# Which engine makes the low parts of the streamed weights in a four-layer decoder trunk

## Chip, core and metric

The kernel runs on one core of one Trainium2 chip. The metric is the device time of one execution in microseconds (us); lower is better.

## What is computed

Four layers act on one sequence of 256 tokens with 1024 features in float32. Each layer normalises its input, runs a token mixer of its own kind (sparse attention in three branches, differential, dilated and stick-breaking attention), gates the result with a SiLU path, projects it back, normalises it again and adds it to the running state.

```python
def reference(x, norm_pre, norm_post, a_w_in, a_w_out, ...):
    h = x
    for i in range(DEPTH):                       # DEPTH = 4
        m, j = i % N_MIXERS, i // N_MIXERS
        u = rms_norm(h, norm_pre[i])
        if m == 0:
            y = nsa_mixer(u, a_w_in[j], a_w_out[j], ...)
        elif m == 1:
            y = diff_mixer(u, b_w_in[j], b_w_out[j], ...)
        elif m == 2:
            y = dilated_mixer(u, c_w_in[j], c_w_out[j])
        else:
            y = stick_mixer(u, d_w_in[j], d_w_out[j])
        h = h + rms_norm(y, norm_post[i])
    return h
```

Every mixer ends in `(o * silu(z)) @ w_out`, and q, k, v and z come from `u @ w_in`. These projections are most of the matrix work.

## The kernel before

**Weights as a stream.** All projection weights come from HBM in 164 pieces of at most 128 x 1024 float32, in the order of their use (the list `seq`). Layer 0 has its v pieces, its other input pieces, eight pieces of a small network that are not split, and its output pieces; layers 1 to 3 follow with eight v pieces (`b_v`, `c_v`, `d_v`), 20 or 24 further input pieces (`b_t`, ...) and eight output pieces (`b_o`, ...).

**The split.** A float32 product is made of three products of a shorter format (fp32r): an operand is written as a high part plus a low part, and the product low times low is left out. `advance` (L70 to L115) starts the DMA of a piece into one of five `raw` buffers, has ScalarE copy it into the high part `whi` (L106), and then subtracts, `wlo = raw - whi` (L108). The high and low parts lie in eleven buffers each. Which engine makes the subtraction is the choice `on_pool` (L107): VectorE (`DVE`), or GpSimd (`POOL`) for piece 6, for the pieces of the table `POOL2`, and for the fifth and eighth v piece of layers 1 to 3 (`POOLV`). In `POOL2` are six pieces near the end of layer 0 (29, 33, 37, 41, 45 and 49, the last of which is the second v piece of layer 1) and three at the end of layer 3 (152, 156 and 160). Without piece 6 that makes 15 pieces. TensorE multiplies the activations with the parts in `mm3` (L202 to L204) and `nat` (L262 to L264).

**Order of the work.** TensorE's order is written out by hand. On the other engines a scheduler sorts by priority; the splits from piece 12 on have a low one (`LATE`), so that the order of an engine is fixed when the program is built, and depends on which instructions the engine has. An engine works through its list strictly in order.

**From one layer to the next** (three times; "boundary" in what follows). The output projection (`out_proj`) does token block 0, then token block 1. While TensorE works on block 1, block 0 is normalised and transposed. When block 1's projection is done, a chain of small steps follows: squares on ScalarE (L417), mean (L421) and product (L423) on VectorE, a power on GpSimd (L157), the addition to `h` (L435, two halves), again squares (L173 on ScalarE, L174 on VectorE), L176, again a power on GpSimd (L157), scaling (L183, two halves), and then the transposes on TensorE (L190), after which ScalarE and VectorE write `uth` and `utl` (L193, L194). Meanwhile TensorE does the v projection of block 0 for the next layer (16 steps of three matmuls, L262 to L264), and the transposes of block 1 are placed before its fourteenth and before its last step (`with_trans`). The eight v pieces are split in this same stretch.

**Layer 3.** A unit handles two heads: scores on TensorE, L1031 on VectorE, three ScalarE passes (L1032, L998), L1035, two scans (L1038) and L1040 on VectorE, an exponential on ScalarE, transposes on TensorE (L303), copies to SBUF on ScalarE (L148), and the product with v on TensorE (L319, L322). VectorE does the two heads one after the other, with splits in between.

Of the kernel before, what the change touches and what calls it, by code (L numbers as in the profile page):

```python
# [17 lines left out]
PSUM = bass.MemoryType.PSUM  # L18
# [8 lines left out]
KO = (0, 4, 1, 5, 2, 6, 3, 7)  # L27
X1AT, SUMAT, UAT, T1AT, WARM = 4, 1, 3, 4, 12
POOLED = (6,)
POOL2 = (*range(29, 50, 4), *range(152, 164, 4))  # L30
POOLV = (("_v", 4), ("_v", 7))
CHAIN, T0, T1, V0, V1 = 400, 6, 4, 3, 1


# [5 lines left out]
def trunk(ctx, tc, I, out):  # L40
# [7 lines left out]
    ps = ctx.enter_context(tc.tile_pool(name="ps", bufs=1, space=PSUM))  # L48
    ctx.enter_context(tc.manual_schedule(engines={mybir.EngineType.PE}))

# [1 line left out]
    seq = []  # L52

    def add(name, *idx, split=True):
# [14 lines left out]
    raw, parts = {}, {}  # L69

    def advance(most=len(seq)):
        while True:
            while st["load"] < min(len(seq), st["split"] + NS - st["held"] + max(0, min(3, 8 - st["split"]))):
                i = st["load"]
                if i == X1AT:
                    nc.sync.dma_start(h[:, 1, :], I["x"][1])
                _, k, c = seq[i][0].shape
                if 5 <= i < 8:
                    if i == 5:
                        st["extra"] = big.tile([128, 3, 560], F32, name="oT")  # L80
                    t = st["extra"][:, i - 5, :]
                else:
                    t = wts.tile([128, 1024], F32, name="raw", bufs=NS)[:, :k * c]
                t = t.rearrange("p (k c) -> p k c", k=k)
                dma = nc.sync.dma_start(t, seq[i][0])
                if i == 7:
                    st["dma"] = dma.ins
                raw[i] = t
                st["load"] += 1
            i = st["split"]  # L90
            if i >= st["load"] or st["parts"] >= NH or i >= min(most, st["most"]):
                return
            t = raw.pop(i)
            st["split"] += 1
            if not seq[i][1]:
                parts[i] = t
                st["held"] += 1
                continue
            _, k, c = seq[i][0].shape
            hi, lo = [wts.tile([128, 1024], F32R, name=n, bufs=NH)[:, :k * c].rearrange("p (k c) -> p k c", k=k)  # L100
                      for n in ("whi", "wlo")]
            with ExitStack() as after:
                after.enter_context(tc.high_priority(offset=LATE if i >= 12 else 0))
                for ins in st["after"]:
                    after.enter_context(tc.issue_after(ins))
                ACT.activation(hi, t, AF.Copy)  # L106
                on_pool = i in POOLED or i in POOL2 or (i > 8 and seq[i][2] in POOLV)  # L107
                lo_of = (POOL if on_pool else DVE).tensor_tensor(lo, t, hi.bitcast(F32), op=OP.subtract)  # L108
                if i == max(POOLED):
                    st["pool"] = lo_of.ins  # L110
                elif not on_pool:
                    st["lo"] = lo_of.ins
            parts[i] = (hi, lo)
            st["parts"] += 1
# [7 lines left out]
            parts.pop(i)  # L122
            st["parts" if seq[i][1] else "held"] -= 1

# [1 line left out]
    def bcast_load(dst, name, l):  # L126
        src = I[name]
        nc.scalar.dma_start(dst, bass.AP(tensor=src.tensor, offset=src.offset + l * D, ap=[[0, 128], [1, D]]))
# [5 lines left out]
    nc.scalar.dma_start(gcol, I["gain0"])  # L134
    ident = const.tile([128, 128], F32, name="ident")

# [1 line left out]
    cnt = {"ev": 0}  # L138

    def evac(dst, src, eng=None):  # L140
# [67 lines left out]
    ready = {}  # L208

    def fill():  # L210
        """Work of the queue between two attention steps, spread evenly over the steps that are left."""
        n = -(-(len(fq) - plan["keep"]) // max(1, plan["slots"]))
        plan["slots"] -= 1
        for _ in range(max(0, n)):
            pop()
# [7 lines left out]
            pop()  # L223

    def need(i):
        """Projection i and a little more, so that its result has left PSUM."""
        while fq and (i not in ready or plan["count"] < ready[i] + 6):
            pop()

    def push_proj(use, q=fq, idx=None):  # L230
        """Two streamed pieces -> [128 cols, 2, 256 tokens] in PSUM, given to use()."""
        t = {}
        idx = idx or take(2)

        def step(c, k):
            if c == 0 and k == 0:
                t["o"] = ps.tile([128, 2, 256], F32, name="mm", bufs=NMM)
            wh, wl = parts[idx[c]]
            mm3(t["o"][:, c, :], wh[:, k, :], wl[:, k, :], uT[0][:, k, :], uT[1][:, k, :], k == 0, k == 7)
            if k == 7:  # L240
                free(idx[c])
                if c == 1:
                    use(t["o"])
                advance()

        for c in range(2):
            for k in range(8):
                q.append(lambda c=c, k=k: step(c, k))

    def nat(stat, b, idx, c0, c1, use, last, ko=range(8)):  # L250
        """Natural orientation: token block b, columns c0:c1 of 8 kt in the pieces idx; a list of steps."""
        t = {}

        def step(k):
            if k == 0:
                t["o"] = ps.tile([128, 512], F32, name="mm", bufs=NMM)
            o = t["o"][:, 0:c1 - c0]
            i, j = divmod(k, 8 // len(idx))
            wh, wl = parts[idx[i]]
            bs = slice(b * 128, (b + 1) * 128)  # L260
            sh, sl = stat[0][:, ko[k], bs], stat[1][:, ko[k], bs]
            PE.matmul(o, sh, wh[:, j, c0:c1], start=k == 0, stop=False)  # L262
            PE.matmul(o, sl, wh[:, j, c0:c1], start=False, stop=False)  # L263
            PE.matmul(o, sh, wl[:, j, c0:c1], start=False, stop=k == 7)  # L264
            if k == 7:
                use(o)
                if last:
                    free(*idx)
                    advance()

        return [lambda k=k: step(k) for k in range(8)]

    def with_trans(steps, trans, t0, t1):
        """The transposes of the other token block go in near the end of the steps."""
        n = len(steps)
        if trans:
            steps[n - t0:n - t0] = trans[0:1]
            steps[n + 1 - t1:n + 1 - t1] = trans[1:2]
        for f in steps:
            f()  # L280

    def v_proj(trans):
        """Token block 0 first; trans: the transposes that bring in token block 1."""
        v = big.tile([128, 2, D], F32, name="v")
        idx = take(8)
        for b in range(2):
# [19 lines left out]
        return t  # L306

    def scores(S, kT, qT, kc, qc, halves):
        """S[j] [128, 384] = q block 0 x keys 0..127 | q block 1 x keys 0..255, heads on partition halves."""
        for b in range(2):  # L310
            for j in halves:
                r = slice(64 * j, 64 * j + 64)
                PE.matmul(S[j][:, 128 * b:128 * b + 128 * (b + 1)], qT[r, qc, b * 128:(b + 1) * 128],  # L313
                          kT[r, kc, 0:128 * (b + 1)], start=True, stop=True)

    def pv_pair(o, PT, v, cols, first, last):
        """o [128 = 2 heads x 64, 256 tokens] += V^T P^T; PT[j], cols[j] for the two heads."""
        for j in range(2):
            PE.matmul(o[64 * j:64 * j + 64, :], v[:, 0, cols[j]:cols[j] + 64], PT[j][:, 0:256],  # L319
                      start=first, stop=False)  # L320
# [2 lines left out]
                      start=False, stop=last)  # L323

    class Gate:
        """g = o * silu(z) in two fp32r parts; column tiles 2i, 2i+1 once o and z are both there."""

        def __init__(self, scale, silu):
            self.scale, self.silu, self.w, self.o, self.gh = scale, silu, {}, set(), None
# [32 lines left out]
                DVE.tensor_tensor(lo, g, hi.bitcast(F32), op=OP.subtract)  # L362

        def open(self):
            """The scores are done: the query and key tiles take the two parts of g."""
            self.gh = [big.tile([128, 8, 256], F32R, name=n) for n in ("qT", "kT")]
            for i in range(self.ready):
                self.split(i)

    def pipeline(units, ga, pattern, keep=8, tail=3):  # L370
        """units: (fronts, backs) of closures; the fronts of unit n + 1 go with the backs of unit n."""
        n = len(units)
        order = []
        for i in range(n + 1):
# [100 lines left out]
        return [a.ins, v.ins]  # L475

    def start(steps):
        """Layer 0's first projection as x and the weights come in; steps[k]: both column chunks of k, block 0."""
        make_identity(nc, ident)
        uT[0] = big.tile([128, 8, 256], F32R, name="uth")  # L480
        uT[1] = big.tile([128, 8, 256], F32R, name="utl")
# [68 lines left out]
    nc.sync.dma_start(cq, I["qscale"])  # L550
    causal = mask_tile("causal")

    # =================== layer 0: native sparse attention ===================
    SLA = slopes_of(16)
    pos = const.tile([128, 2, 16], F32, name="pos")
    nc.sync.dma_start(pos, I["pos"])
# [153 lines left out]
    CS, PTC = {}, {}  # L710

    def cmp_front(g):
        """Compressed branch, the 4 heads of a group at once."""
        need(g)
        sc = ps.tile([128, 512], F32, name="S", bufs=NSB)
        for b in range(2):
# [91 lines left out]

    trans = out_proj(pipeline([nsa_unit(p) for p in range(8)], ga, "FFBFBBB"), 0)

    # =================== layer 1: differential attention ===================
    SLB = slopes_of(8)
    LI = 0.8 - 0.6 * math.exp(-0.3)
    lamt = work.tile([128, 384], F32, name="P", bufs=8)[:, 0:256].rearrange("p (a b) -> p a b", a=4)
# [101 lines left out]

    trans = out_proj(pipeline([diff_unit(hd) for hd in range(8)], ga, "FBFBFBB"), 1)

    # =================== layer 2: dilated attention ===================
    SLC = slopes_of(12)  # L920
    with tc.issue_after(st["pool"]):
        masks = [mask_tile("near"), mask_tile("by4"), mask_tile("by16")]
# [62 lines left out]

    trans = out_proj(pipeline([dilated_unit(hg) for hg in range(4)], ga, "FFBFBB"), 2)

    # =================== layer 3: stick-breaking attention ===================
    with tc.issue_after(st["pool"]):
        mstrict = mask_tile("strict")  # L990
        zero = const.tile([128, 256], F32, name="zero")
# [64 lines left out]

# [1 line left out]
def _nat(w, nk=(2, 2, 2, 2), nc_=512):  # L1058
    """[1024, C] -> pieces [128, kt, nc_] for each column chunk, split over kt."""
    import numpy as np  # L1060
    w = w.reshape(8, 128, w.shape[1])
    res = []
# [6 lines left out]


def _tr(w):
    """[1024, C] -> [C / 128, 128, 8, 128]."""
    import numpy as np
    c = w.shape[1]
    return np.ascontiguousarray(w.reshape(8, 128, c // 128, 128).transpose(2, 1, 0, 3))
# [60 lines left out]
```

## Time and profile before

| | us |
|---|---|
| three runs | 620.87, 619.18, 620.79 (median 620.79) |
| span of the profiled execution, first to last instruction | 618.9 |
| TensorE busy (matmuls) | 591.9 |
| VectorE busy | 428.2 |
| ScalarE busy | 348.4 |
| GpSimd busy | 68.0 |
| low parts on VectorE: 138 in the group of the page, mean | 1.24 |
| low parts on GpSimd: 15 in the group, mean | 2.47 |

The profile tells only the span of its execution. The runs lie 0.3 to 2.0 us above it, which is what lies around the first and the last instruction. Times in the profile are counted from the span's start. A busy time is a sum over the whole span, and an engine can be late in one place and idle in most others; so the waits and the order of time are read for the places in question.

### The profile page before, as it was taken

The page shows a single profiled execution, that of the slowest core. Times are in us where ns is not written, and L with a number is a line of the kernel's source. Part 1 is how long each engine was busy: PE and PEld are TensorE (multiplying, and loading weights), DVE is VectorE, ACT ScalarE, POOL GpSimd, SP SyncE. Part 2 cuts the span into 40 slices and gives each one's busy share as a digit, 9 for nine tenths or more (in the row PEclk, how much of TensorE's full clock was granted, in tenths as well). Part 3 has the DMA queues.
Part 4 walks back from the last instruction along what each step waited for, and adds up shares of the span by engine and source line. Part 5 has one row for each costly group of instructions (what it writes and reads, how often), then busy time and mean ns, then how long its engine had stood idle before and what let it go on. Part 6 is the DMA issues. An engine that isn't in the chain of part 4 may idle for free.

```text
span 618.9 us, 10516 instructions
## 1 busy us (share of the span) xinstructions
PE 591.9 (96%) x3930; PEld 501.6 (81%) x3930; DVE 428.2 (69%) x927; ACT 348.4 (56%) x756; POOL 68.0 (11%) x98
## 2 busy tenths in 40 slices
PE   7999999999999899999999899999998999889896
PEld 6995867666788699999988699998986898778884
DVE  6870698675826786776857785657557868878842
ACT  6730687565725275666635374456442766677930
POOL 1400113010012200001402200000013000111000
PEclk9999999999999899999999899999998999999998
DMA  8653847221141486443451396433505773221011
GB/s 302 242 203 137 283 161 237 70 69 35 44 169 34 137 299 246 137 137 126 147 171 38 134 323 222 141 132 103 166 39 169 252 259 136 102 104 69 1 35 68
DMA packets 27779, 90.96 MB, mean 147 GB/s; under 512 B 4560, under 2 KB 5200, under 8 KB 27728
## 3 DMA queue, kind: packets, MB, share of 16 engines
q1 hardware_dynamic: 26144, 86.09, 40.3%
q10 hardware_dynamic: 1584, 4.20, 2.1%
q8 instruction: 31, 0.51, 0.3%
q14 instruction: 20, 0.16, 0.1%
HBM read 89.22 MB, written 1.05 MB: 146 GB/s over the span
## 4 chain that ended last, share of the span: by engine, by line
PE 75%; DVE 9%; ACT 7%; issue 5%; POOL 2%; DMA 1%; SPq 0%; POOLq 0%; DVEq 0%; ACTq 0%
PE mm L202 15%; PE mm L203 12%; PE mm L204 12%; PE mm L263 6%; PE mm L262 6%; PE mm L264 6%; PE S L765 4%; PE S L313 3%; DVE wlo L108 3%; ACT whi L106 3%; PE pt L303 2%; PE o L319 2%; PE o L641 2%; ACT P L998 1%; DVE P L1038 1%
## 5 line engine op out<-in xcount | busy, mean ns | idle before, releaser
L202 PE MATMUL mm<-uth,whi 128*128 128x256 f32 x736 | 222.8, 303 | 0.0
L203 PE MATMUL mm<-utl,whi 128*128 128x256 f32 x736 | 207.8, 282 | 0.0
L204 PE MATMUL mm<-uth,wlo 128*128 128x256 f32 x736 | 207.6, 282 | 0.0
L108 DVE TENSOR_TENSOR wlo<-raw,whi 128x1024 fp32r<-128x1024 f32 (+1 forms) x138 | 169.5, 1240 | 53.0 <-ACT whi L106 52.1
L106 ACT ACTIVATE whi<-raw 128x1024 fp32r<-128x1024 f32 (+1 forms) x153 | 156.9, 1044 | 79.6 <-PE mm L203 40.1
L202 PEld LDWEIGHTS mm<-uth,whi 128*128 128x128 f32 x736 | 140.2, 191 | 36.2 <-issue 36.1
L203 PEld LDWEIGHTS mm<-utl,whi 128*128 128x128 f32 x736 | 140.6, 191 | 0.1
L204 PEld LDWEIGHTS mm<-uth,wlo 128*128 128x128 f32 x736 | 140.3, 191 | 0.0
L108 POOL TENSOR_TENSOR wlo<-raw,whi 128x1024 fp32r<-128x1024 f32 x15 | 37.1, 2471 | 249.1 <-ACT whi L106 246.6
L262 PE MATMUL mm<-whi,qT 128*128 128x512 f32 x128 | 50.4, 394 | 0.0
L263 PE MATMUL mm<-whi,kT 128*128 128x512 f32 x128 | 49.9, 390 | 0.0
L264 PE MATMUL mm<-wlo,qT 128*128 128x512 f32 x128 | 49.9, 390 | 0.0
L264 PE MATMUL mm<-wlo,uth 128*128 128x512 f32 (+1 forms) x112 | 43.6, 389 | 0.8 <-DVE wlo L108 0.8
L263 PE MATMUL mm<-whi,utl 128*128 128x512 f32 (+1 forms) x112 | 43.6, 389 | 0.9 <-DVE utl L474 0.9
L262 PE MATMUL mm<-whi,uth 128*128 128x512 f32 (+1 forms) x112 | 44.2, 394 | 0.0
L296 DVE CUSTOM_DVE_ANT_0 P<-S,mask 128x128 f32<-128x128 f32 (+1 forms) x96 | 30.5, 349 | 13.1 <-PE S L765 10.9
L998 ACT ACTIVATE P<-P 128x384 f32<-128x384 f32 x48 | 23.8, 517 | 18.4 <-DVE P L1040 17.6
L417 ACT ACTIVATE junk<-mm 128x512 bf16<-128x512 f32 x16 | 9.5, 595 | 39.5 <-PE mm L264 39.5
L298 ACT ACTIVATE P<-P,mxa 128x128 f32<-128x128 f32 (+1 forms) x64 | 28.5, 448 | 5.5 <-DVE mxa L296 5.4
L148 ACT ACTIVATE PT<-pt 128x384 f32<-128x384 f32 x58 | 25.3, 479 | 6.1 <-PE pt L303 6.1
L264 PEld LDWEIGHTS mm<-wlo,qT 128*128 128x128 f32 x128 | 24.0, 188 | 5.1
L262 PEld LDWEIGHTS mm<-whi,qT 128*128 128x128 f32 x128 | 24.1, 188 | 4.7
(203 smaller groups left out, 832.4 us busy)
## 6 DMA issues: line engine op xcount, KB each, us to landing
raw<-in_a_t_dram SPq DMA_DIRECT2D x24, 512.0 KB, 4.3
raw<-in_b_t_dram SPq DMA_DIRECT2D x24, 512.0 KB, 4.8
raw<-in_d_t_dram SPq DMA_DIRECT2D x24, 512.0 KB, 4.8
raw<-in_c_t_dram SPq DMA_DIRECT2D x20, 512.0 KB, 4.5
raw<-in_w_dram SPq DMA_DIRECT2D x8, 512.0 KB, 4.6
raw<-in_a_o_dram SPq DMA_DIRECT2D x8, 512.0 KB, 4.4
raw<-in_b_v_dram SPq DMA_DIRECT2D x8, 512.0 KB, 3.5
raw<-in_b_o_dram SPq DMA_DIRECT2D x8, 512.0 KB, 3.5
```

Source lines behind the costliest of these rows:

```text
L106: ACT.activation(hi, t, AF.Copy)
L108: lo_of = (POOL if on_pool else DVE).tensor_tensor(lo, t, hi.bitcast(F32), op=OP.subtract)
L148: ACT.activation(dst, src, AF.Copy)
L202: PE.matmul(o, sh, mh, start=first, stop=False)
L203: PE.matmul(o, sh, ml, start=False, stop=False)
L204: PE.matmul(o, sl, mh, start=False, stop=last)
L262: PE.matmul(o, sh, wh[:, j, c0:c1], start=k == 0, stop=False)
L263: PE.matmul(o, sl, wh[:, j, c0:c1], start=False, stop=False)
L264: PE.matmul(o, sh, wl[:, j, c0:c1], start=False, stop=k == 7)
L296: DVE.tensor_tensor_reduce(out=P[:, c0:c1], in0=S, in1=mask[:, c0:c1], scale=-slope, scalar=BIG, op0=OP.add, op1=OP.min, accum_out=mx)
L298: ACT.activation(P[:, c0:c1], P[:, c0:c1], AF.Exp, bias=mx, scale=-1.0, accum_out=l)
L998: return ACT.activation(*a, **k)
```

## The change

The tables `POOL2` and `POOLV` go, and `on_pool` holds for piece 6 alone. The 15 other subtractions are issued on VectorE. Nothing else of the computation differs (comments and docstrings went too, so that line numbers of the changed kernel are 2 lower from L32 on).

```diff
 POOLED = (6,)
-POOL2 = (*range(29, 50, 4), *range(152, 164, 4))
-POOLV = (("_v", 4), ("_v", 7))
...
                 ACT.activation(hi, t, AF.Copy)
-                on_pool = i in POOLED or i in POOL2 or (i > 8 and seq[i][2] in POOLV)
+                on_pool = i in POOLED
                 lo_of = (POOL if on_pool else DVE).tensor_tensor(lo, t, hi.bitcast(F32), op=OP.subtract)
```

The orders of TensorE and of the DMA queue are the same in both. VectorE's list at the first boundary, from the second pair of L194 to the scaling, was before (tu is the scaled state, poh and pnh the two norms, utl the low part of the transposed state):

```order
L194 TENSOR_TENSOR utl<-pt,uth 128x4x128 x2
L108 TENSOR_TENSOR wlo<-raw,whi 128x1024 x2
L421 SCALAR_TENSOR_TENSOR poh<-ss,poh 128x1
L423 TENSOR_TENSOR tu<-mm,oT 128x512
L435 SCALAR_TENSOR_TENSOR h<-tu,poh,h 128x512 x2
L108 TENSOR_TENSOR wlo<-raw,whi 128x1024
L174 ISA junk,pn_2243<-h 128x512
L174 ISA pn_2243 128x1
L146 COPY v<-mm 128x512
L176 SCALAR_TENSOR_TENSOR pnh<-pn_2242,pn_2243 128x1
L820 TENSOR_SCALAR subg<-subg 128x1
L183 SCALAR_TENSOR_TENSOR tu<-h,pnh,oT 128x512 x2
```

and is now (line numbers of the changed kernel, 2 lower):

```order
L192 TENSOR_TENSOR utl<-pt,uth 128x4x128 x2
L106 TENSOR_TENSOR wlo<-raw,whi 128x1024 x3
L419 SCALAR_TENSOR_TENSOR poh<-ss,poh 128x1
L421 TENSOR_TENSOR tu<-mm,oT 128x512
L433 SCALAR_TENSOR_TENSOR h<-tu,poh,h 128x512 x2
L106 TENSOR_TENSOR wlo<-raw,whi 128x1024
L172 ISA junk,pn_2243<-h 128x512
L172 ISA pn_2243 128x1
L144 COPY v<-mm 128x512
L174 SCALAR_TENSOR_TENSOR pnh<-pn_2242,pn_2243 128x1
L106 TENSOR_TENSOR wlo<-raw,whi 128x1024
L181 SCALAR_TENSOR_TENSOR tu<-h,pnh,oT 128x512 x2
```

Two subtractions joined the list: the fifth v piece as one of three ahead of L421, and the eighth between L176 and L183. The other two boundaries changed in the same way.

VectorE's list in the middle of layer 3, one unit, from its L1031 pair to the next, was before (P are the two heads' score tiles, kT a copied projection):

```order
L1031 TENSOR_TENSOR P<-S,mask 128x384 x2
L1035 SCALAR_TENSOR_TENSOR P<-P 128x384
L1038 SCALAR_TENSOR_TENSOR P<-P,zero 128x128
L1038 SCALAR_TENSOR_TENSOR P<-P,zero 128x256
L1040 TENSOR_TENSOR P<-P 128x384
L108 TENSOR_TENSOR wlo<-raw,whi 128x1024
L146 COPY kT<-mm 128x512
```

and is now:

```order
L1029 TENSOR_TENSOR P<-S,mask 128x384 x2
L106 TENSOR_TENSOR wlo<-raw,whi 128x1024
L1033 SCALAR_TENSOR_TENSOR P<-P 128x384
L1036 SCALAR_TENSOR_TENSOR P<-P,zero 128x128
L1036 SCALAR_TENSOR_TENSOR P<-P,zero 128x256
L1038 TENSOR_TENSOR P<-P 128x384
L144 COPY kT<-mm 128x512
L1033 SCALAR_TENSOR_TENSOR P<-P 128x384
L106 TENSOR_TENSOR wlo<-raw,whi 128x1024
```

The first subtraction moved up behind the L1031 pair, and the one that GpSimd made stands between L1035 and the scans of the second head.

## Rows read from the trace of the kernel before

**Rows 1.** Page, part 1: busy us, share of the span, instructions

```profile
PE 591.9 (96%) x3930; PEld 501.6 (81%) x3930; DVE 428.2 (69%) x927; ACT 348.4 (56%) x756; POOL 68.0 (11%) x98
```

**Rows 2.** Page, part 5: busy, mean ns of one; idle before, releaser

```profile
L108 POOL TENSOR_TENSOR wlo<-raw,whi 128x1024 fp32r<-128x1024 f32 x15 | 37.1, 2471 | 249.1 <-ACT whi L106 246.6
```

**Rows 3.** Waits of TensorE, whole span: us in total, times, longest

```profile
PE pt L190 <- DVE tu L183: 6.9, 3, 2.3
PE o L319 <- ACT PT L148: 5.5, 5, 1.6
...
PE S L765 <- DVE cs L726: 0.6, 1, 0.6
```

**Rows 4.** Stretches: PE, PEld, DVE, ACT, POOL busy (count), clock, DMA, GB/s

```profile
206.00:214.00 8.00, 5.43 (x22) 4.02 (x21) 4.39 (x9) 0.89 (x2) 0.55 (x1) 0.79 0.41 129
...
471.00:480.00 9.00, 6.44 (x25) 4.80 (x24) 4.93 (x10) 1.79 (x5) 0.55 (x1) 0.81 0.35 116
...
522.00:575.00 53.00, 48.98 (x388) 42.94 (x387) 44.31 (x68) 37.65 (x76) 7.55 (x3) 1.00 0.27 97
```

**Rows 5.** Timeline of TensorE, first boundary: start, us, instruction, [idle before]

```profile
206.33 0.39 PE L263 MATMUL mm<-whi,utl 128*128 128x512 f32 x1
207.00 0.50 PE L264 MATMUL mm<-wlo,uth 128*128 128x512 f32 x1 [0.28 <-DVE wlo L108]
209.78 1.08 PE L190 MATMUL pt<-ident,tu 128*128 128x128 f32 x4 [2.28 <-DVE tu L183]
```

**Rows 6.** Timeline of VectorE, first boundary

```profile
187.87 1.41 DVE L435 SCALAR_TENSOR_TENSOR h<-tu,poh,h 128x512 f32<-128x512 f32 x2
...
196.96 1.22 DVE L108 TENSOR_TENSOR wlo<-raw,whi 128x1024 fp32r<-128x1024 f32 x1 [0.26 <-ACT whi L106]
198.86 2.67 DVE L108 TENSOR_TENSOR wlo<-raw,whi 128x1024 fp32r<-128x1024 f32 x1 [0.67 <-ACT whi L106]
201.46 0.15 DVE L421 SCALAR_TENSOR_TENSOR poh<-ss,poh 128x1 f32<-128x1 f32 x1
...
202.27 3.54 DVE L435 SCALAR_TENSOR_TENSOR h<-tu,poh,h 128x512 f32<-128x512 f32 x2
205.74 1.21 DVE L108 TENSOR_TENSOR wlo<-raw,whi 128x1024 fp32r<-128x1024 f32 x1
...
208.08 0.14 DVE L176 SCALAR_TENSOR_TENSOR pnh<-pn,pn 128x1 f32<-128x1 f32 x1
...
208.89 1.41 DVE L183 SCALAR_TENSOR_TENSOR tu<-h,pnh,oT 128x512 f32<-128x512 f32 x2 [0.60 <-POOL pnh L157]
...
215.29 5.77 DVE L108 TENSOR_TENSOR wlo<-raw,whi 128x1024 fp32r<-128x1024 f32 x5 [0.26 <-ACT whi L106]
```

**Rows 7.** Timeline of GpSimd, first boundary

```profile
197.96 2.50 POOL L108 TENSOR_TENSOR wlo<-raw,whi 128x1024 fp32r<-128x1024 f32 x1 [7.04 <-ACT whi L106]
...
202.20 2.40 POOL L108 TENSOR_TENSOR wlo<-raw,whi 128x1024 fp32r<-128x1024 f32 x1
```

**Rows 8.** Chain that ended last, around the first boundary: start, us, what

```profile
193.09 0.44 PE pt L190 x4
193.53 0.23 PE mm L262
...
209.78 1.08 PE pt L190 x4
210.87 0.43 PE mm L262
```

**Rows 9.** Timelines of VectorE and of TensorE in layer 3

```profile
528.52 2.73 DVE L1035 SCALAR_TENSOR_TENSOR P<-P 128x384 f32<-128x384 f32 x1
...
548.37 0.55 DVE L1035 SCALAR_TENSOR_TENSOR P<-P 128x384 f32<-128x384 f32 x1
...
537.09 0.43 PE L319 MATMUL o<-PT,v 128*64 128x256 f32 x1 [1.60 <-ACT PT L148]
...
546.28 0.43 PE L319 MATMUL o<-PT,v 128*64 128x256 f32 x1 [0.32 <-ACT PT L148]
```

## Prediction

> **What bounds the kernel now.** The page's first part says that TensorE is busy 96% of the span and VectorE 69% [rows 1], so at first sight a few subtractions more or less on VectorE should be hidden. The second view is therefore TensorE's own list of waits: where it stood still, and for whom [rows 3]. Two entries are large. Three times it waited for VectorE's scaled state L183 before the transposes L190, 6.9 us in all and 2.3 at the longest, so about the same at each of the three boundaries. Five times in layer 3 it waited for ScalarE's copies of the transposed scores, 5.5 us in all. Layer 0 has one entry of 0.6 us. GpSimd's subtractions are named nowhere in that list, so the third view is the time around the waits, engine by engine.
>
> At the first boundary TensorE starts L263 at 206.33 and the next matmul, which wants a low part, only at 207.00; then the transposes wait until 209.78 [rows 5]. The matmuls go at a distance of 0.23 us [rows 8], so TensorE lost 0.67 - 0.23 = 0.44 us and then 209.78 - 207.00 - 0.23 = 2.55 us. Directly after this wait the matmuls go at 0.43 us instead of 0.23, and the four transposes take 1.08 instead of 0.44 [rows 8]. The stretch table gives the reason: a mean granted clock of 0.79 from 206 to 214 and 0.81 at the third boundary [rows 4], a mix of full clock (2.4 GHz) and half.
>
> Why L183 is late is in VectorE's timeline [rows 6] beside GpSimd's [rows 7]. A subtraction takes 1.22 us, but the one at 198.86 took 2.67, while GpSimd made one from 197.96 to 200.46. The pair L435 takes 1.41 us at 187.87, but 3.54 at 202.27, while GpSimd made another from 202.20 to 204.60. The stretched VectorE instructions end about one ordinary duration after GpSimd's: they stood still as long as GpSimd was at it. In layer 3 it is the same: an L1035 takes 0.55 us at 548.37 and 2.73 at 528.52 [rows 9], in a stretch where GpSimd had three subtractions with 7.55 us [rows 4].
>
> The Trainium skill says the same of the mechanism ("SBUF — State Buffer", the section on the two separate sides of SBUF): VectorE instructions with two SBUF inputs, or in a two-port mode, and GpSimd instructions share a pair of ports as an exclusive lock, and the later one waits for the whole of the other. The trace agrees with it in the two stretched pairs above.
>
> So a subtraction on GpSimd (2.47 us, 15 of them [rows 2]) does not relieve VectorE. It stops it for some 2 us where VectorE wants the ports, to save it 1.14: five in a row take 5.77 us, and (5.77 - 1.22) / 4 = 1.14 us is the distance [rows 6].
>
> **The change part by part.** TensorE's and the DMA queue's orders stay. GpSimd loses 15 instructions, VectorE gains 15 x 1.14 = 17.1 us. What counts is where they stand.
>
> *A boundary, step by step.* The three subtractions ahead of L421 start at 196.96 as before; ScalarE had the third high part ready by 198.86 [rows 6], so they follow each other: 196.96 + 3 x 1.14 = 200.38 for L421, before 201.46. From L421 to L435 it was 202.27 - 201.46 = 0.81 (GpSimd's power lies in it and stays), so L435 starts at 201.19. The pair takes 1.41 rather than 3.54: 202.60. From the next subtraction (205.74) to L176 (208.08) it was 2.34, so L176 starts at 204.94. Now the moved subtraction stands in front of L183. Before, VectorE was idle there for 0.60 us, waiting for GpSimd's power [rows 6]; so 1.14 us covers this wait and costs the rest: L183 starts 0.07 + 1.14 us after L176, at 206.15, before 208.89. L183 to the transposes was 209.78 - 208.89 = 0.89: they can start at 207.04, which is **2.74 us** earlier.
>
> TensorE is there at that time: the low part for which it waited from 206.56 comes from the subtraction that now starts at 202.60 and ends at 203.8, so TensorE goes through and is done at 206.33 + 2 x 0.23 = 206.79. It waits 0.25 us rather than 0.44 + 2.55. The last moved subtraction ends by 206.2 and its piece is wanted two steps later, so it stops nothing.
>
> *The clock.* Between the first transposes and the second there are two steps, six matmuls. At the low clock five of them went at 0.43 and the transposes took 1.08: 5 x 0.20 + 0.64 = **1.64 us** lost. The waits of 1.60 us in layer 3 [rows 9] lie in a stretch whose clock is 1.00 [rows 4]. A wait of 0.25 is far below those, so I take it that the clock stays up and the 1.64 us come back; the bounds are 0 and 1.64 a boundary. A boundary gives 2.74 + 1.64 = 4.38 us, three give **13.1** (8.2 if the clock still falls). Behind it TensorE is busy without a break in either kernel, so nothing gives the time back.
>
> *Layer 3.* Two kinds of waits before L319: 1.60 us, three of the five, and 0.32, the other two (3 x 1.60 + 2 x 0.32 = 5.4, the entry of 5.5). The three long ones come a unit after one of GpSimd's three subtractions. A hold costs 2.73 - 0.55 = 2.18 us of VectorE, the added subtraction 1.14, and some of it lies where VectorE waits for ScalarE after L1031 anyway, since the order now puts a subtraction there. Net VectorE is 1.0 us a unit faster or better. From both sides: 0 if the new places cost what the holds did, 5.5 if all waits go. I take the short kind for all: 3 x (1.60 - 0.32) = **3.8 us**.
>
> *Layer 0.* Six GpSimd subtractions, and only one wait of TensorE, 0.6 us for L726. Its cause is a hold two instructions earlier. The order there changes over some 200 rows, with bursts of three to four subtractions; TensorE has its next scores ready far ahead in all but this place. Bounds: 0.6 gained, 1.1 lost for one subtraction that comes in front of a score tile. I take **0.6** gained. *DMA:* a raw buffer comes free with the low part. That of the eighth v piece does so at 206.2 instead of 204.6, those of the others earlier; the piece loaded into it is wanted after the 11 us v projection of block 1, so I cost this at nothing.
>
> Sum: 13.1 + 3.8 + 0.6 = **17.5 us**. The profiled span of 618.9 becomes 601.4; the median of the runs lies 1.9 above that span, so the forecast is **603.3 us**.
>
> **The rivals.**
>
> *The clock falls all the same,* or the transposes still wait for something that I don't see: the boundary gives 2.74. For it: some 0.25 us of wait remains. Against: the longer waits in layer 3. 620.8 - 8.2 - 3.8 - 0.6 = 608.2 us.
>
> *VectorE is the bound of layer 3.* It is busy 44.31 of 53.00 us there [rows 4]; with three subtractions more it could set the pace, and the layer would lose 3 x 1.14 = 3.4 us rather than gain 3.8. Against: that busy time holds 3 x 2.18 = 6.5 us of standing still; without it and with the three subtractions it is 41.2. It would give 620.8 - 13.1 - 0.6 + 3.4 = 610.5 us. The Trainium skill has this as a rule ("Perfetto Trace Analysis", section on optimising Scalar and DVE operations): where VectorE is saturated, handing work to ScalarE or even GpSimd may make sense; it adds that between VectorE and GpSimd the shared port may spoil it.
>
> *Slower: the holds are not GpSimd's doing.* If L435 and the others stretch for another reason that merely falls together with GpSimd (a transfer, ScalarE), the stretches stay and the subtractions are added. At a boundary 1.14 comes in front of L421, and 0.54 (1.14 less the idle 0.60) in front of L183: 3 x 1.68 = 5.0, and in layer 3 3.4: 629 us. It decides where L435 at a boundary still takes 3.5 us. Against: every stretched one in rows 6 and 9 ends with GpSimd's, and the same line without GpSimd is short.
>
> *No change:* the chain is shortened, but TensorE is then held by a wait just behind, and by as much; or the bursts in layer 0 eat the gain. Some 620 us. Nothing in the lists shows such a wait.
>
> **How the numbers follow.** Forecast 0.77; clock 0.08; layer 3 0.08; slower 0.04; no change 0.03. All waits in layer 3 gone gives 620.8 - 13.1 - 5.5 - 0.6 = 601.6, and the scatter of the runs is 1 us to either side: the low end is 600. The high end takes in the clock and layer 3: 611. A change of 0.3% is 1.9 us, about what a measurement of this kernel can tell. Faster by more 0.93, within 0.03, slower 0.04.
>
> **What would show it.** L435 takes 1.4 us at all three boundaries; L190 starts less than half a microsecond after the matmul before it; the clock is 1.00 in the boundary stretches; of 6.9 us of waiting for L183 under 1 is left; the waits before L319 are all of the short kind. The prediction is wrong if L435 stays at 3.5 us, if the clock still falls, or if TensorE has a new wait in layer 0 on VectorE.

## The result and the profile after

The changed kernel takes **603.84 us** (median of 4 runs, 603.22 to 604.47) against 620.83 (4 runs, 619.18 to 620.91): a ratio of 0.974, 95% interval 0.972 to 0.976. The forecast was 603.3. A second measurement on another chip, beside the experiments below, gave 603.16 against 620.79, 0.972 (0.970 to 0.973). One run of experiment 3 (643.54 us) was slow throughout, at a mean clock of 0.848, and enters no comparison. Lines of the changed kernel are two lower than before: the low part is L106, the scaled state L181, the transposes L188.

The page's first part, which answers to [rows 1]:

```profile
PE 586.6 (97%) x3930; PEld 499.1 (83%) x3930; DVE 421.0 (70%) x942; ACT 349.1 (58%) x756; POOL 33.3 (6%) x83
```

VectorE has 15 instructions more (942 against 927) and is busy 7.2 us less. The 17.1 us of added subtractions are there; what is gone is more, time in which VectorE counted as busy and stood still.

TensorE's waits over the whole span, which answer to [rows 3]: us in total, times, longest.

```profile
PE pt L188 <- DVE tu L181: 1.6, 3, 0.6
PE o L317 <- ACT PT L146: 1.6, 5, 0.5
```

The wait for the scaled state fell from 6.9 to 1.6, that in layer 3 from 5.5 to 1.6, and the wait of the scores in layer 0 is not in the list any more. The three boundary stretches and the one of layer 3, as in [rows 4] (PE, PEld, DVE, ACT, POOL busy, granted clock, DMA):

```profile
204.00:212.00 8.00, 7.44 (x38) 5.91 (x37) 5.44 (x9) 3.18 (x5) 1.47 (x1) 1.00 0.39 133
343.00:351.00 8.00, 8.00 (x39) 6.60 (x38) 6.34 (x7) 6.18 (x9) 0.00 (x0) 1.00 0.43 126
465.00:474.00 9.00, 9.00 (x44) 7.49 (x43) 6.83 (x8) 6.98 (x9) 0.00 (x0) 1.00 0.43 136
507.00:560.00 53.00, 51.64 (x413) 45.51 (x411) 45.34 (x77) 40.31 (x82) 0.00 (x0) 1.00 0.32 100
```

The clock is at its upper level (2.4 GHz) at the boundaries, where it was 0.79 and 0.81 on average. The second and the third stretch begin just behind the start of the transposes (341.96 and 464.68), so the waits ahead of these, 0.69 and 0.71 us, are not in their rows. In layer 3 TensorE is busy 51.64 of 53 us, where it was 48.98, and VectorE 45.34, so VectorE is not the bound there. VectorE's timeline at the first boundary, which answers to [rows 6]:

```profile
196.38 3.50 DVE L106 TENSOR_TENSOR wlo<-raw,whi 128x1024 fp32r<-128x1024 f32 x3 [0.26 <-ACT whi L104]
199.79 0.15 DVE L419 SCALAR_TENSOR_TENSOR poh<-ss,poh 128x1 f32<-128x1 f32 x1
...
200.61 1.41 DVE L433 SCALAR_TENSOR_TENSOR h<-tu,poh,h 128x512 f32<-128x512 f32 x2
201.94 1.22 DVE L106 TENSOR_TENSOR wlo<-raw,whi 128x1024 fp32r<-128x1024 f32 x1
...
204.29 0.15 DVE L174 SCALAR_TENSOR_TENSOR pnh<-pn,pn 128x1 f32<-128x1 f32 x1
204.36 1.22 DVE L106 TENSOR_TENSOR wlo<-raw,whi 128x1024 fp32r<-128x1024 f32 x1
206.02 1.41 DVE L181 SCALAR_TENSOR_TENSOR tu<-h,pnh,oT 128x512 f32<-128x512 f32 x2 [0.45 <-POOL pnh L155]
```

The three subtractions take 3.50 us in a row and the pair 1.41, as forecast. One thing is not: from L174 to the scaled state it was to be 1.21 us, and it is 206.02 - 204.29 = 1.73. GpSimd's timeline says why:

```profile
200.03 0.55 POOL L155 TENSOR_TENSOR poh<-poh,nhalf 128x1 f32<-128x1 f32 x1 [9.68 <-DVE poh L419]
204.52 1.47 POOL L155 TENSOR_TENSOR pnh<-pnh,nhalf 128x1 f32<-128x1 f32 x1 [3.94 <-DVE pnh L174]
```

The power on one column takes 0.55 us in the first row. In the second, where VectorE began the moved subtraction 0.16 us earlier (204.36), it takes 1.47 and ends 0.4 us after VectorE's. The hold works in the other direction too. So TensorE still waits a little, as its timeline shows ([rows 5] has the rows of before):

```profile
205.97 0.39 PE L262 MATMUL mm<-wlo,uth 128*128 128x512 f32 x1
206.92 0.63 PE L188 MATMUL pt<-ident,tu 128*128 128x128 f32 x4 [0.56 <-DVE tu L181]
```

That is 206.92 - 205.97 - 0.23 = 0.72 us lost, where 0.25 was forecast and 2.55 + 0.44 lay before.

**Where the time went.** All of these kernels give TensorE the same 3930 matmuls in the same order, so the start of one of them, less its start in the kernel before, is a running account. Its change over each part of the program, in us:

| part | forecast | changed kernel | again, other chip | that part alone on VectorE |
|---|---|---|---|---|
| start, to 73 us | 0 | +1.2 | -0.1 | |
| layer 0 | -0.6 | -1.8 | -1.8 | -1.8 (experiment 2) |
| first boundary | -4.4 | -3.6 | -3.7 | -3.7 (experiment 1) |
| second | -4.4 | -3.9 | -3.9 | -3.9 |
| third | -4.4 | -3.8 | -3.9 | -3.8 |
| layer 3 | -3.8 | -4.2 | -4.2 | -4.2 (experiment 3) |
| whole | -17.5 | -16.1 | -17.4 | |

The start differs between executions: this profile has a mean clock of 0.58 from 11.5 to 15.6 us, the second profile of the same kernel and that of before have 1.00 there.

### The profile page after: what moved, and what is told of

The parts are those of the page before. It is cut to its first block, busy times and chain, and to the rows that moved or that the text cites. A ratio compares the mean times of both kernels' runs of the same rounds, so it can differ in the third digit from the quotient of the medians.

```text
span 602.8 us, 10496 instructions
## 1 busy us (share of the span) xinstructions
PE 586.6 (97%) x3930; PEld 499.1 (83%) x3930; DVE 421.0 (70%) x942; ACT 349.1 (58%) x756; POOL 33.3 (6%) x83
## 3 DMA queue, kind: packets, MB, share of 16 engines
HBM read 89.22 MB, written 1.05 MB: 150 GB/s over the span
## 4 chain that ended last, share of the span: by engine, by line
PE 77%; DVE 9%; ACT 5%; issue 4%; DMA 2%; POOL 1%; SPq 0%; POOLq 0%; DVEq 0%; ACTq 0%
PE mm L200 15%; PE mm L201 12%; PE mm L202 12%; PE mm L261 6%; PE mm L262 6%; PE mm L260 6%; PE S L763 4%; DVE wlo L106 4%; PE S L311 3%; PE pt L301 3%; PE o L317 2%; ACT whi L104 2%; PE o L639 2%; ACT P L996 1%; DVE P L1036 1%
## 5 line engine op out<-in xcount | busy, mean ns | idle before, releaser
L106 DVE TENSOR_TENSOR wlo<-raw,whi 128x1024 fp32r<-128x1024 f32 (+1 forms) x153 | 182.4, 1208 | 47.8 <-ACT whi L104 46.4
L261 PE MATMUL mm<-whi,utl 128*128 128x512 f32 (+1 forms) x112 | 42.2, 376 | 1.0 <-DVE utl L472 1.0
L260 PE MATMUL mm<-whi,uth 128*128 128x512 f32 (+1 forms) x112 | 42.6, 380 | 0.0
L262 PE MATMUL mm<-wlo,uth 128*128 128x512 f32 (+1 forms) x112 | 42.1, 376 | 0.0
L261 PEld LDWEIGHTS mm<-whi,kT 128*128 128x128 f32 x128 | 24.1, 188 | 4.7
```

## The experiments

The theory: GpSimd's subtraction and VectorE's instructions exclude each other; at a boundary this makes the scaled state late, TensorE waits, and its clock falls behind the wait. Rivals: what cost time is that others wait for GpSimd's slow result, or the order that VectorE got; or any activity of GpSimd does it.

### 1 to 3: one part of the change at a time

Each is the kernel before, with a part of the subtractions on VectorE.

```diff
 experiment 1, boundaries
-POOLV = (("_v", 4), ("_v", 7))
+POOLV = ()
 experiment 2, layer 0
-POOL2 = (*range(29, 50, 4), *range(152, 164, 4))
+POOL2 = (*range(152, 164, 4),)
 experiment 3, layer 3
-POOL2 = (*range(29, 50, 4), *range(152, 164, 4))
+POOL2 = (*range(29, 50, 4),)
```

> Only the subtractions of the fifth and eighth v piece at the three boundaries go to VectorE; the nine others stay on GpSimd. Theory (GpSimd's subtraction holds VectorE, so the scaled state comes late, TensorE waits, and its clock falls): by the prediction 3 x 4.38 = 13.1 us less, so 607.7; by the distance between the two traces at the boundaries (3.7, 3.7 and 3.8 us) 11.2 less, so 609.6. The pair L435 takes 1.4 us at each boundary, the clock there is 1.00, and the waits of layer 3 before L319 stay at 5.5 us. Rival 'the clock falls all the same': 8.2 less, 612.6. Rival 'the gain is mainly layer 3's and layer 0's': above 614.

> Only the six subtractions of layer 0 go to VectorE. By the prediction 0.6 us less, 620.2. By the distance between the two traces, in which TensorE's position moved by 1.6 us over layer 0, 1.6 less, 619.2. Rival (the bursts on VectorE cost as much as the holds): no change, 620.8, or up to 0.5 more. The one wait of 0.6 us of the scores for VectorE in layer 0 should be gone in the first two cases.

> Only the three subtractions of layer 3 go to VectorE. By the prediction 3.8 us less, 617.0; by the distance between the two traces over layer 3 4.1 less, 616.7: TensorE's waits before L319 fall from 5.5 us to about 1.6. Rival (VectorE sets the pace of layer 3, and the layer only gains because the boundary behind layer 2 sends its state earlier): 0 to 3.4 us more, 621 to 624. If the parts are independent, the three differences of these kernels add up to the whole, 17 us.

Against 620.14 us of the kernel before on that chip (26 runs, 617.25 to 622.36):

| on VectorE | us | ratio, 95% interval |
|---|---|---|
| boundaries | 610.83 | 0.985 (0.982 to 0.988) |
| layer 0 | 617.70 | 0.997 (0.995 to 0.999) |
| layer 3 | 615.40 | 0.993 (0.990 to 0.996) |

By the ratios that is 9.5, 2.0 and 4.4 us, 16.0 together. The first is 1.2 us above the expected 609.6; its profile has the 11.4 us at the boundaries, but starts 1.4 us later, as the first profile of the change does. The second is 1.5 us below the expected 619.2; in its profile the clock stayed up at the first boundary, which is 1.4 us, though the wait there was as long as before. The third was run once more for its trace.

> The kernel with only layer 3's three subtractions on VectorE once more, for its trace: before L319 TensorE waits 1.6 us in all instead of 5.5, the waits at the boundaries stay at 6.9 us, and the time is 616 to 617 us (first measured 616.2).

It took 614.94 us against 621.07, 0.990 (0.988 to 0.992), which is 6.1 us; its profile has 4.2 in layer 3 and 1.6 at the second boundary, where the clock did not fall this time, though the wait was as long as before. TensorE's waits in it:

```profile
PE pt L190 <- DVE tu L183: 6.9, 3, 2.3
PE o L319 <- ACT PT L148: 1.6, 5, 0.5
```

The waits of layer 3 go without those of the boundaries. So layer 3's gain is its own, and "it only gains because the state comes earlier" falls. The account part by part, in which that clock and the start are left out, gives 11.4, 1.8 and 4.2 us (the table above), together as much as the 17.4 of the whole in the second profile of the change. To about 0.1 us the three parts are independent and nothing else is in the gain.

Layer 0 gained three times the forecast. TensorE's timeline at one place in the kernel before:

```profile
96.96 0.70 PE L765 MATMUL S<-kT,qT 64*128 64x256 f32 x2
98.29 0.67 PE L765 MATMUL S<-kT,qT 64*128 64x256 f32 x2 [0.63 <-DVE cs L726]
```

and the same four matmuls with layer 0's six on VectorE:

```profile
95.72 0.70 PE L765 MATMUL S<-kT,qT 64*128 64x256 f32 x4
```

From the first start to the last end it was 98.29 + 0.67 - 96.96 = 2.00 us, and is 0.70: 1.3 us, of which the list of waits had shown 0.6. The cause stands on VectorE ahead of L726: an L786, which takes 0.35 us, took 2.48 while GpSimd made a subtraction from 93.43 to 95.81. VectorE and GpSimd in the kernel before:

```profile
93.48 2.48 DVE L786 TENSOR_SCALAR P<-P,la 128x256 f32<-128x256 f32 x1
```

```profile
93.43 2.38 POOL L108 TENSOR_TENSOR wlo<-raw,whi 128x1024 fp32r<-128x1024 f32 x1 [12.50 <-ACT whi L106]
```

Two other groups of four scores, at 75.44 and 81.47, shrink from 1.30 to 0.85 and from 1.47 to 0.87 and stood in no list. Ahead of each of them VectorE had a stretched instruction too: a subtraction of 2.23 us at 72.12, and at 79.13 an L734 of 1.82 us, which takes 0.17 in experiment 2. The three groups gain 2.35 us together. Some 0.55 is lost again by 145 us, 0.46 of it at a fourth group, which takes 1.45 us instead of 0.99: TensorE comes to it 2.53 us earlier (142.13 for 144.66), VectorE's L726 only 2.08 (142.68 for 144.76).

### 4: the holds alone, on the changed kernel

GpSimd gets a subtraction of the same size whose result nobody reads, where it had the fifth and the eighth v piece.

```diff
+POOLV = (("_v", 4), ("_v", 7))
...
+    spare = const.tile([128, 1024], F32, name="spare")
...
+                if i > 8 and seq[i][2] in POOLV:
+                    POOL.tensor_tensor(spare[:, 0:k * c], hi.bitcast(F32).rearrange("p k c -> p (k c)"),
+                                       hi.bitcast(F32).rearrange("p k c -> p (k c)"), op=OP.subtract)
```

> The changed kernel, with six subtractions of the same size added on GpSimd at the boundaries (the high part less itself, into a tile that nobody reads). VectorE, TensorE and ScalarE have the changed kernel's instructions in the same order, and nobody waits for GpSimd's new results. Theory (GpSimd holds VectorE through what both use at the same time): the holds are back, at each boundary one L435 pair or one subtraction takes about 2 us more than alone, the scaled state comes 2 to 4 us later, the clock falls to half behind the wait; 3 x (2 to 5.5) us more than 603.8, so 610 to 620. Rival (what cost time was that TensorE and VectorE had to wait for GpSimd's result, which takes 2.4 instead of 1.2 us, or the order in which the scheduler then put VectorE's work): 603.8, with L435 at 1.4 us.

It took **619.02 us**, 0.998 (0.997 to 1.000) of the kernel before: the boundaries' gain is gone, and more, though all real work stands where the changed kernel has it. VectorE's, GpSimd's and TensorE's timelines at the first boundary:

```profile
195.10 5.20 DVE L108 TENSOR_TENSOR wlo<-raw,whi 128x1024 fp32r<-128x1024 f32 x3 [0.26 <-ACT whi L106]
...
201.03 3.04 DVE L438 SCALAR_TENSOR_TENSOR h<-tu,poh,h 128x512 f32<-128x512 f32 x2
```

```profile
196.09 1.99 POOL L110 TENSOR_TENSOR spare<-whi 128x1024 f32<-128x1024 f32 x1 [7.03 <-ACT whi L106]
...
200.96 1.90 POOL L110 TENSOR_TENSOR spare<-whi 128x1024 f32<-128x1024 f32 x1
```

```profile
205.25 0.51 PE L267 MATMUL mm<-wlo,uth 128*128 128x512 f32 x1 [0.41 <-DVE wlo L108]
208.96 1.08 PE L193 MATMUL pt<-ident,tu 128*128 128x128 f32 x4 [3.20 <-DVE tu L186]
```

The subtractions take 1.70 us more and the pair 1.63, 3.33 together; by the account TensorE is 3.3 us later at the transposes, and 5.9 behind the boundary, so 2.6 are the clock's. Nobody reads the spare tile, and VectorE has the changed kernel's order: for the boundaries the rival of the slow result falls, and so does that of the order, and with them the rival of the prediction in which the stretches are not GpSimd's doing.

The idle subtractions stand at the boundaries only. In layers 0 and 3, 6 of the 17.4 us, experiments 2 and 3 take the holds away and change VectorE's order in one step. That the holds are what cost time there is read from the stretched instructions; no run separates them from the order.

### 5 and 8: what GpSimd must do to hold VectorE

At the same places, instead of the subtraction:

```diff
 experiment 5: writes only
+                    POOL.tensor_copy(spare[:, 0:1], hi.bitcast(F32)[:, 0, 0:1])
+                    for _ in range(3):
+                        POOL.memset(spare, 0.0)
 experiment 8: one input read
+                    POOL.tensor_copy(spare[:, 0:k * c], hi.bitcast(F32).rearrange("p k c -> p (k c)"))
```

> The changed kernel, with GpSimd filling an unused tile of 128x1024 three times at each place where the run before had the unused subtraction; GpSimd only writes there, and reads one column for the start. If every activity of GpSimd holds VectorE's instructions with two inputs, the holds are back and the time is that of the run with the unused subtractions, 619.0 us, or more if the fills last longer. If GpSimd's work holds VectorE only where it reads two inputs as the subtraction does, the L435 pair and the subtractions stay as short as in the changed kernel: 603.8 us. One or two stretched instructions only: between the two.

> The changed kernel with an unused copy of the high part on GpSimd at the six places where the earlier runs had an unused subtraction (619.0 us) or unused fills (605.0 us): one input is read instead of two or none. If reading anything is what makes GpSimd hold VectorE, the pair L435 and the subtractions are stretched by about the copy's own duration, and the time is above 606 us, by how much depends on that duration: the wait of 1.9 us that the eighth piece alone gave cost 1.3 us a boundary, so 607 to 612. If only an instruction with two inputs holds, as the subtraction has, the pair takes 1.4 us and the time is 603 to 605.

The fills: 605.01 us, 0.975 (0.973 to 0.977). VectorE and then GpSimd at the first boundary:

```profile
200.81 1.42 DVE L439 SCALAR_TENSOR_TENSOR h<-tu,poh,h 128x512 f32<-128x512 f32 x2 [0.69 <-POOL poh L161]
```

```profile
200.23 0.55 POOL L161 TENSOR_TENSOR poh<-poh,nhalf 128x1 f32<-128x1 f32 x1
200.73 0.18 POOL L110 COPY spare<-whi 128x1 f32<-128x1 f32 x1
200.97 2.98 POOL L112 MEMSET spare<- 128x1024 f32 x3
```

The fills run through the pair, and it takes 1.42 as alone (the copy of one column is there to time their start). What is left, 605.01 - 603.16 = 1.85 us, is GpSimd's own queue: the power starts 0.87 us after L425 (199.36), behind the first three fills, against 0.23 without them; 3 x 0.64 = 1.9.

The copies: 610.50 us, 0.983 (0.981 to 0.985). VectorE, GpSimd:

```profile
200.81 2.17 DVE L437 SCALAR_TENSOR_TENSOR h<-tu,poh,h 128x512 f32<-128x512 f32 x2
```

```profile
200.73 1.04 POOL L110 COPY spare<-whi 128x1024 f32<-128x1024 f32 x1
```

The pair starts 0.08 us behind the copy and takes 0.76 us more than alone; the copy still had 200.73 + 1.04 - 200.81 = 0.96 to go. One input is enough to hold, writing is not. The Trainium skill states it so ("SBUF — State Buffer", the section on the two separate sides): a VectorE instruction with two SBUF inputs is only held by a GpSimd instruction that reads SBUF, and whichever starts first has the ports for its whole length. The runs agree with the first part here, and the power of 1.47 us with the second.

### 7: the eighth piece alone on GpSimd

The edit is to the kernel before, so that of the 15 subtractions only the three of the eighth pieces stay on GpSimd.

```diff
-POOL2 = (*range(29, 50, 4), *range(152, 164, 4))
-POOLV = (("_v", 4), ("_v", 7))
+POOL2 = ()
+POOLV = (("_v", 7),)
```

> As the changed kernel, but the eighth v piece's subtraction stays on GpSimd at the three boundaries; that of the fifth is on VectorE. It splits the boundary's gain. By the prediction's steps the first three subtractions then end 1.08 us earlier than before and the pair L435 is still held for 2.1, so of 2.74 us a boundary keeps 1.1 and the clock still falls: 3 x (3.7 - 1.1) = 7.8 us more than the changed kernel, 611.6. Rival (the eighth piece on GpSimd spares VectorE the subtraction in front of the scaled state and costs little): 604 to 606.

607.01 us, 0.978 (0.976 to 0.980), where 611.6 was expected: the chain was priced rightly, the clock not. By the account the wait ahead of the transposes gives back 1.05 us at the first boundary against the kernel before (expected 1.1). But the clock stays up. TensorE's timeline and the stretch:

```profile
204.89 0.39 PE L264 MATMUL mm<-wlo,uth 128*128 128x512 f32 x1
207.06 0.63 PE L190 MATMUL pt<-ident,tu 128*128 128x128 f32 x4 [1.79 <-DVE tu L183]
```

```profile
204.00:213.00 9.00, 7.21 (x36) 5.76 (x35) 6.23 (x12) 4.05 (x6) 0.55 (x1) 1.00 0.30 107
```

A wait of 207.06 - 204.89 - 0.23 = 1.94 us leaves it at the upper level, at all three boundaries. With the copies of experiment 8 the wait is about 2.3 us at each boundary, and the stretches are these:

```profile
205.00:213.00 8.00, 5.85 (x31) 4.61 (x30) 5.45 (x9) 3.24 (x5) 1.46 (x1) 1.00 0.43 131
342.00:350.00 8.00, 5.84 (x30) 4.65 (x29) 5.39 (x8) 3.60 (x5) 1.46 (x1) 1.00 0.37 127
466.00:475.00 9.00, 6.86 (x28) 5.32 (x28) 4.85 (x8) 2.77 (x4) 1.46 (x1) 0.81 0.34 117
```

There it fell at one of the three. At the 2.55 us of the kernel before it fell at seven of nine boundaries (that kernel, and experiments 2 and 3, which keep its boundaries), and with experiment 4's wait of 208.96 - 205.25 - 0.23 = 3.48 us at all three.

### 6: the eighth piece behind the scaled state

On the changed kernel, the subtraction of the eighth piece is taken from its place in front of L181 and put behind it, so that neither it nor the power holds the other.

```diff
-            DVE.scalar_tensor_tensor(u[:, q * 512:(q + 1) * 512], h[:, b, q * 512:(q + 1) * 512], r,
+            tu = DVE.scalar_tensor_tensor(u[:, q * 512:(q + 1) * 512], h[:, b, q * 512:(q + 1) * 512], r,
...
+        if b:
+            st["after"], st["most"] = [tu.ins], st["next"] + 8
+            advance()
...
-                st["after"], st["most"] = [a.ins, v.ins], len(seq) if b else st["next"] + 8
+                st["after"], st["most"] = [a.ins, v.ins], len(seq) if b else st["next"] + 7
```

> The changed kernel, with one thing moved: at each boundary the subtraction of the eighth v piece stands behind the scaled state L183 instead of in front of it on VectorE. Theory (in the changed kernel VectorE's subtraction holds GpSimd's power, which takes 1.46 us instead of 0.55, so that the scaled state starts 1.7 us behind L176): the power is back at 0.55, the scaled state starts about 1.0 us earlier, and the wait of TensorE of 0.69 us in front of the transposes goes: 3 x 0.5 to 0.7 less, so 601.7 to 602.3 against 603.8. Rival (the subtraction cost nothing there, since TensorE waits for something else, or the low part of the eighth piece is then late for its step): 603.8 or a little more, with a wait for that low part in TensorE's list.

> The changed kernel itself, for the comparison with the three others on the same chip: 603.8 us by every theory.

**600.91 us** (4 runs, 600.79 to 601.70) against 603.16 of the changed kernel on the same chip (603.08 to 603.21) and 620.79 before: 0.968 of before (0.966 to 0.970), a little better than expected, and the fastest of all. VectorE, GpSimd, TensorE:

```profile
202.86 0.15 DVE L174 SCALAR_TENSOR_TENSOR pnh<-pn,pn 128x1 f32<-128x1 f32 x1
203.67 1.42 DVE L181 SCALAR_TENSOR_TENSOR tu<-h,pnh,oT 128x512 f32<-128x512 f32 x2 [0.66 <-POOL pnh L155]
205.00 1.22 DVE L106 TENSOR_TENSOR wlo<-raw,whi 128x1024 fp32r<-128x1024 f32 x1
```

```profile
203.09 0.55 POOL L155 TENSOR_TENSOR pnh<-pnh,nhalf 128x1 f32<-128x1 f32 x1 [3.94 <-DVE pnh L174]
```

```profile
204.54 0.39 PE L265 MATMUL mm<-wlo,uth 128*128 128x512 f32 x1
204.77 0.60 PE L191 MATMUL pt<-ident,tu 128*128 128x128 f32 x4
```

The power is back at 0.55, the scaled state starts 0.81 us after L174, and the transposes follow the matmul at the ordinary 0.23. The move gave 603.16 - 600.91 = 2.25 us. It takes two things away at once. The scaled state starts 0.92 us nearer to L174 (0.81 for 1.73): 0.52 is what the held power had added to the forecast 1.21, the other 0.40 is the subtraction's own place in front. A boundary gives 4.4, 4.6 and 4.6 us here. That this is close to the 4.38 worked out for the change is partly chance: at the first boundary it is 2.99 of waiting and 1.42 of clock, where 2.74 and 1.64 were forecast.

## Why the prediction was right, and where its terms were off

The time (603.3 against 603.84 and 603.16) was right, and so was the mechanism; three of its terms were off by more than the sum shows.

- **Boundary, the chain: 2.74 us forecast with the 0.44 before it among them, 2.29 measured** in the second profile of the change (0.45 in the wait for the low part and 1.84 ahead of the transposes). The steps down to L176 hold. The one that failed is "L183 starts 0.07 + 1.14 us after L176": it took GpSimd's power as free beside the subtraction. The prediction had the exclusion, and used it in one direction only. It measured 1.73 us, which is 0.5 us more at each boundary; in experiment 6, with the subtraction behind, the power takes 0.55 again and the wait is gone. So two of the signs that the prediction named did not come: the transposes start 0.95 us after the matmul before them (under 0.5 was named), and 1.6 us of waiting for the scaled state are left (under 1).
- **Boundary, the clock: 1.64 forecast, 1.4 to 1.6 measured.** That the clock would stay up was right, and its wait was 0.72, not 0.25. The argument from layer 3's waits of 1.60 carried further than was used: 1.94 was harmless too. The rival "the clock falls all the same" falls; its other half, that the transposes still wait for something unseen, came true in small: of the 0.7 us that they wait, 0.5 are the held power's.
- **Three boundaries: 13.1 forecast, 11.4 measured.** Behind a boundary nothing gives the time back: the account is flat between them to 0.02 us in the second profile.
- **Layer 3: 3.8 forecast, 4.2 measured.** All five waits are now of the short kind (1.6 in all, 0.5 at the longest). The rival "VectorE is the bound" falls with VectorE's 45.34 of 53 us and experiment 3.
- **Layer 0: 0.6 forecast, 1.8 measured.** The mis-sized step is reading the loss off the list of waits. The list had one row of 0.6 us; the distances between the starts of the scores had 2.35, of which 0.55 was lost again. Nor is the hold two instructions ahead of L726, as the prediction has it: it is the L786 at 93.48, six rows ahead.
- **Slower, and no change:** the pair takes 1.41 us, not 3.5; experiment 4 brings the stretches back with GpSimd's work alone.
- **The base: 1.9 us between span and time.** In every run on record the time lies 1.67 to 1.79 us above its own span, so what lies outside the span is 0.1 to 0.2 us less than was added; the rest of the 1.9 is the scatter of the runs.

Errors of +1.7, -1.2 and -0.4 us cancelled. The sum was better than its parts, and that it met the time within 0.6 us is luck in part.

## What to carry to other kernels

Work that is handed to GpSimd to relieve a busy VectorE can cost it more time than it saves: a subtraction of 2.4 us held VectorE for about 2 and saved it 1.14. Look in the timeline for instructions of one shape with two durations, and for what GpSimd reads at that time; look for it in both directions, since a 1.2 us instruction on VectorE holds a small one on GpSimd that the critical chain wants. And size a wait by the distances between starts, not by the list of waits alone.

## What the hardware showed that was not expected

- The hold is mutual: a power on one column took 0.55 us, and 1.46 to 1.47 where a 1.22 us subtraction of VectorE had begun just before it.
- Three fills by GpSimd (2.98 us, no input) did not lengthen VectorE's pair at all; a copy (1.04 us, one input) lengthened it by 0.76.
- Not only VectorE's instructions with two tensor inputs were held: an L734 (TENSOR_SCALAR, 128x8) took 1.82 us in layer 0 under GpSimd's subtraction of 78.00 to 80.93, and 0.17 without it in experiment 2.
- After waits of 2.3 and 2.55 us TensorE's clock fell at some boundaries and not at others. The kernel before has three waits of that kind, and its 26 runs beside experiments 1 to 4 scatter over 617.3 to 622.4 us. The time goes with the mean clock of the run: three runs at 0.997 took 617.3 to 617.5 us, eight at 0.986 and 0.987 took 621.3 to 622.4. The changed kernel's four in the second measurement, at 0.997 to 0.999, lie within 0.13. Where in a run the clock fell is known for the profiled ones only.
